# A hybrid decoder step on one core: the down projection's operands split where they are made and brought back by GpSimd's queue

## The chip, the core and the metric

The program runs on one core of a Trainium2 chip. TensorE (PE) multiplies, VectorE (DVE) and ScalarE (ACT) do the elementwise work, GpSimd (POOL) a little of it, and SyncE (SP) issues the transfers between DRAM (HBM) and the core's on-chip memory (SBUF). Products gather in eight banks of PSUM. The metric is the device time of one launch in microseconds (us). The kernel before took 1199.58 us, the median of three runs (1198.73 to 1200.3).

## The reference

One layer of a hybrid decoder, on 1088 tokens (1024 of a prompt and 8 sequences of 8 sampled tokens), 1024 features:

```python
h = rmsnorm(x, norm_mix_pre)
mix = concat([conv(h), pool(h), hgrn2(h), conformer(h)]) @ w_out      # four mixers on the columns of h @ w_in
x = x + rmsnorm(mix, norm_mix_post)
h = rmsnorm(x, norm_ffn_pre)
ff = (silu(h @ w_gate) * (h @ w_up)) @ w_down                         # 1024 -> 2816 -> 1024
x = x + rmsnorm(ff, norm_ffn_post)
```

Everything is float32. The change lies in the last product: its inner dimension of 2816 is 22 tiles of 128 hidden features.

## The kernel before, in words

**Split operands.** A float32 product is made of three faster ones. Each operand is split into a high part (a float32r copy, which ACT makes: CAST) and a low part (the rest, which DVE or POOL makes by a subtraction: TENSOR_TENSOR, line 65 through the helper `TT`), and high by high, high by low and low by high are added in PSUM. Names that end in `h` and `l` (`xh0`, `xl0`) are the two parts of the FFN's input, `wop` holds both parts of a weight tile, `raw` a weight tile as loaded.

**Stages.** Phase 1 (to about 380 us of the trace) is the input projection and the mixers. Phase 2 is the output projection, the norms, and the hidden tiles 16, 17 and 18 for all tokens by plain products (`plain`, line 1288, products on line 1297). A planner writes the order of phase 2 by hand: each step of DVE's work is a generator that tells its cost in us, and `hook` places as much of it under a stretch of products as fits; the steps in `bulk` fill what is left, and `due` holds small steps that have to be done at once.

Phase 3a makes the other hidden tiles, 0 to 15 and 19 to 21, with Strassen's seven products in Winograd's form (`strassen`, products on line 1388), tile after tile, in two streams `pr` = 0 and 1 (each half of the tokens), whose products alternate on PE. One tile is 168 matmuls. Tiles 0 to 15 form eight pairs: after the odd tile of a pair, `pair_sums` (line 1430) makes the seven operands that the down projection's own Strassen products need and stores each to DRAM (`hx`), whole, 128 x 272 per stream. Tiles 16 to 21 go whole to `hd`. In this phase a scheduler orders each engine's instructions.

Phase 3b (`down2`, products on line 1593) is the down projection of the eight pairs in four groups `g` of two pairs, each group in four steps `j` of 84 matmuls, so 16 steps. A group needs 14 operands (`x_item`): the operand is loaded from `hx` by SP's queue into one of three `raw` tiles of 128 x 544, ACT copies the high part into the operand tile, and POOL subtracts the low part (DVE does for half of group 0). In the same stage DVE makes the weights of the next step (`prep_ws`) and adds the products from PSUM to the sums (`acc`, `t`, `x`). Operand tiles lie where the FFN's input lay (`xh0` to `xl7`) and in a pool `px` of 9; `room` lists them, and a tile goes back into `room` when the last product of its group that reads it is issued. Last, the tiles 16 to 21 of `hd` are loaded in chunks and split in the same manner (`h_items`), and are multiplied by plain products (line 1481), with the final norm under them. In phase 3b the order of PE, DVE, ACT and POOL is the order in which the code is written: each `next` is a product, and the `xs.step()` or `hs.step()` behind it is one operand.

## Time and profile before

| what | value |
|---|---|
| time, median of 3 runs | 1199.58 us |
| span of the profiled execution | 1193.7 us |
| what lies around the span (the difference) | 5.9 us |
| busy: PE / DVE / ACT / POOL | 1153.1 / 885.4 / 451.0 / 139.9 us |
| phase 2, about | 380 to 538 us of the span |
| phase 3a, about | 538 to 927 us |
| phase 3b, pairs, about | 927 to 1100 us |
| plain tiles and final norm, about | 1100 to 1194 us |

The span runs from the first to the last instruction of the profiled execution; the page gives no other time of it. A matmul record lasts longer (288 ns) than the distance to the next one, since matmuls are pipelined: the pace is read from the number of matmuls in a stretch, not from their busy time. DVE's records overlap a little too: a 128 x 272 TENSOR_TENSOR shows 0.43 us.

### The profile page before, as it was taken

How to read it: one execution, taken by the hardware profiler on the slowest of the kernel's cores; microseconds unless marked ns; L12 is line 12 of the kernel's file. 1: busy time of each engine (PE TensorE's matmuls, PEld its weight loads, DVE VectorE, ACT ScalarE, POOL GpSimd, SP SyncE). 2: the span in 40 equal slices, each digit the busy share in tenths (PEclk: the TensorE clock that was granted, in tenths of full speed). 3: DMA queues.
4: the chain of work that ended last, by engine and by line, in shares of the span. 5: the costliest groups of instructions: out<-in, count | busy, mean ns of one | idle time of the engine just before them, and what ended most of it. 6: DMA issues, size and time to landing. Idle time of an engine off the chain costs nothing.

```text
span 1193.7 us, 21654 instructions
## 1 busy us (share of the span) xinstructions
PE 1153.1 (97%) x8476; PEld 1116.1 (94%) x8476; DVE 885.4 (74%) x1770; ACT 451.0 (38%) x964; POOL 139.9 (12%) x130
## 2 busy tenths in 40 slices
PE   5999999999999999999999999999999999999995
PEld 4899899998999999999999999999999989999994
DVE  6468979997674678786677576666675679998687
ACT  7534322243264453443333233233334653333321
POOL 1000000000000000000000000000002363447234
PEclk9999999999899999999999999999999999999998
DMA  7011112211135123021323233133234453434732
GB/s 261 34 38 24 36 37 68 41 36 40 30 130 199 39 74 127 24 95 67 115 101 105 70 111 118 60 114 110 91 122 135 141 178 121 137 109 125 259 108 88
DMA packets 93333, 116.89 MB, mean 98 GB/s; under 512 B 23664, under 2 KB 62192, under 8 KB 93232
## 3 DMA queue, kind: packets, MB, share of 16 engines
q1 hardware_dynamic: 93232, 115.52, 30.1%
q8 instruction: 66, 1.08, 0.4%
q14 instruction: 35, 0.29, 0.1%
HBM read 86.61 MB, written 28.88 MB: 97 GB/s over the span
## 4 chain that ended last, share of the span: by engine, by line
PE 81%; DVE 10%; issue 3%; DMA 2%; ACT 2%; POOL 1%; SPq 0%; DVEq 0%; ACTq 0%; POOLq 0%
PE p L1388 30%; PE mm L984 18%; PE p L1116 8%; PE p L1593 7%; PE p L1297 5%; PE p L1481 4%; DVE wop L65 3%; DVE raw L65 2%; PE mm L137 2%; PE sm L798 2%; DVE t L65 1%; DMA raw<-wgu 1%; ACT wop L1007 1%; DVE xl L65 1%; DMA raw<-hx 1%
## 5 line engine op out<-in xcount | busy, mean ns | idle before, releaser
L65 DVE TENSOR_TENSOR wop<-raw,wop 128x512 fp32r<-128x512 f32 (+2 forms) x296 | 210.2, 722 | 137.9 <-ACT wop L1007 127.5
L1007 ACT CAST wop<-raw 128x512 fp32r<-128x512 f32 (+1 forms) x240 | 143.4, 604 | 267.0 <-PE p L1388 151.7
L1388 PE MATMUL p<-xh,wop 128*128 128x272 f32 x1216 | 235.1, 288 | 0.0
L1388 PEld LDWEIGHTS p<-xh,wop 128*128 128x128 f32 x1216 | 193.5, 188 | 0.0
L1388 PE MATMUL p<-t,wop 128*128 128x272 f32 x912 | 179.6, 290 | 1.7 <-DVE u L65 1.6
L984 PE MATMUL mm<-xh,wop 128*128 128x256 f32 (+2 forms) x864 | 178.5, 335 | 0.0
L1388 PE MATMUL p<-xl,wop 128*128 128x272 f32 x608 | 175.6, 289 | 0.0
L1388 PEld LDWEIGHTS p<-t,wop 128*128 128x128 f32 x912 | 145.6, 188 | 2.4 <-DVE u L65 2.4
L984 PEld LDWEIGHTS mm<-xh,wop 128*128 128x128 f32 x864 | 139.5, 190 | 6.6 <-issue 1.1
L1388 PE MATMUL p<-x,wop 128*128 128x272 f32 x456 | 131.4, 288 | 0.0
L1388 PEld LDWEIGHTS p<-xl,wop 128*128 128x128 f32 x608 | 114.4, 188 | 0.0
L1116 PE MATMUL p<-xh,wop 128*128 128x272 f32 x512 | 99.2, 290 | 2.0 <-DVE wop L65 2.0
L984 PE MATMUL mm<-xl,wop 128*128 128x256 f32 (+2 forms) x432 | 99.0, 338 | 0.0
L65 POOL TENSOR_TENSOR x<-raw,x 128x544 fp32r<-128x544 f32 (+3 forms) x18 | 24.9, 1389 | 626.4 <-ACT x L1521 613.1
L65 DVE TENSOR_TENSOR raw<-raw,raw 128x512 f32<-128x512 f32 (+1 forms) x123 | 83.7, 690 | 4.5 <-DMA raw<-wgu 3.3
L1388 PEld LDWEIGHTS p<-x,wop 128*128 128x128 f32 x456 | 85.9, 188 | 0.0
L1593 PE MATMUL p<-xh,wop 128*128 128x272 f32 x456 | 82.1, 288 | 2.3 <-DVE acc L65 1.2
L71 DVE SCALAR_TENSOR_TENSOR y<-u,prm,y 128x1024 f32<-128x1024 f32 (+1 forms) x68 | 82.6, 1224 | 2.2 <-ACT y L570 0.7
L1116 PEld LDWEIGHTS p<-xh,wop 128*128 128x128 f32 x512 | 81.0, 188 | 2.2 <-DVE wop L65 2.2
L1593 PE MATMUL p<-xl,wop 128*128 128x272 f32 x456 | 81.5, 288 | 1.2 <-DVE x L65 0.9
L1297 PE MATMUL p<-xh,wop 128*128 128x272 f32 x384 | 74.1, 289 | 0.0
L1116 PE MATMUL p<-xl,wop 128*128 128x272 f32 x256 | 73.9, 289 | 0.0
(322 smaller groups left out, 2021.0 us busy)
## 6 DMA issues: line engine op xcount, KB each, us to landing
raw<-wgu SPq DMA_DIRECT2D x88, 256.0 KB, 2.7
raw<-hx SPq DMA_DIRECT2D x56, 272.0 KB, 2.7
raw<-win SPq DMA_DIRECT2D x40, 256.0 KB, 3.0
hx<-x SPq DMA_DIRECT2D x64, 136.0 KB, 1.8
raw<-wdn SPq DMA_DIRECT2D x32, 256.0 KB, 2.9
raw<-wdn SPq DMA_DIRECT2D x32, 192.0 KB, 2.9
x<-xT SPq DMA_DIRECT2D x8, 544.0 KB, 6.2
x<-x SPq DMA_DIRECT2D x8, 544.0 KB, 3.0
```

What stands on the lines that cost most here:

```text
L65: (eng or V).tensor_tensor(out, a, b, op)
L71: (eng or V).scalar_tensor_tensor(out=out, in0=a, scalar=s, in1=b, op0=op0, op1=op1)
L137: PE.matmul(ps[c][:, :n], hl[:, wi, kk], X[k][:, o:o + n], start=k == 0 and wi == 0 and X is XH, stop=k == KT - 1 and wi == 1)
L798: PE.matmul(ps[:rows, g * P:(g + 1) * P], kk[:, o:o + rows], qz[hf][:, :, g * 64:(g + 1) * 64], start=True, stop=True, skip_group_check=True)
L984: PE.matmul(ps[c][:, :w], hl[:, wi, kk], X[k][:, o:o + w], start=k == order[0] and wi == 0 and X is XH, stop=k == order[-1] and wi == 1)
L1007: S.copy(hl[:, 0], raw)
L1116: PE.matmul(ps[nt][:, :PW], WO[nt][k // 4][:, wi, kk:kk + P], X[k][:, o:o + PW], start=k == korder[0] and wi == 0 and X is XH, stop=k == k ...
L1297: PE.matmul(ps[r][:, :PW], w[:, wi, (k % 4) * P:(k % 4 + 1) * P], X[k][:, o:o + PW], start=k == 0 and wi == 0 and X is XH, stop=k == KT - ...
L1388: PE.matmul(ps[:, :PW], wop[:, wi, kk * P:(kk + 1) * P], x(kk, xi), start=first and kk == 0 and wi == 0 and xi == 0, stop=kk == 3 and wi == 1,
L1481: PE.matmul(ps[:, :n], wd[:, wi, kk * P:(kk + 1) * P], hops[k][xi][:, o:o + n], start=first and kk == 0 and wi == 0 and xi == 0, stop=not ...
L1593: PE.matmul(ps[:, :PW], ws[name][wi][q], x[:, xi, pr], start=first and q == 0 and wi == 0 and xi == 0, stop=q == 1 and wi == 1, skip_group ...
```

## The change

The program that stores a part now splits it first. `pair_sums` stores the operands of pairs 0 and 1 whole as before, and those of pairs 2 to 7 as two parts: `put_split` has ACT copy the high part into one of three tiles `hi`, has DVE subtract it in place, and SP store both. `hx` and `hd` become twice as wide. `plain` and `strassen` do the same for tiles 16 to 21. In phase 3b an operand of groups 1 to 3 is one transfer of 128 x 1088 (544 KB) from `hx` straight into its operand tile, and each tile of `hd` two such transfers; all of them are issued by POOL's queue. Their `raw` loads by SP, copies on ACT and subtractions on POOL go. `px` has 8 buffers in place of 9, and one operand of group 0 lies in a tile `hx` of another pool. The weights' raw tiles in phase 3b come from `w4` instead of a pool of their own. In phase 2 `put_t1(0)` stands ahead of `split_t(0)`.

```diff
-    px = ctx.enter_context(tc.tile_pool(name="px", bufs=9, side="right", reuse_waits="tile"))
+    px = ctx.enter_context(tc.tile_pool(name="px", bufs=8, side="right", reuse_waits="tile"))
...
                     def post(ps=ps[1], g0=g0, o=o):
-                        hst = T(pm, [P, PW], "sqa", bufs=2)
+                        hst, hi = T(pm, [P, PW], "sqa", bufs=2), T(pm, [P, PW], "hhi", F32R, bufs=2)
                         TT(hst, ps[:, :PW], g0)
-                        SY.dma_start(hd[i][:, o:o + PW], hst)
-                    due.append((0.36, post))
+                        S.copy(hi, hst)
+                        TT(hst.bitcast(F32R), hst, f32(hi), ALU.subtract)
+                        for w, t in enumerate((f32(hi), hst)):
+                            SY.dma_start(hd[i][w][:, o:o + PW], t)
+                    due.append((0.72, post))
...
-    bulk += [split_t(0), put_t1(0), split_t(1)]
+    bulk += [put_t1(0), split_t(0), split_t(1)]
...
+    def put_split(t, to):
+        hi = T(w3, [P, PW], "hi", F32R, bufs=3)
+        S.copy(hi, t)
+        TT(t.bitcast(F32R), t, f32(hi), ALU.subtract)
+        for dst, src in zip(to, (f32(hi), t)):
+            SY.dma_start(dst, src)
...
-            SY.dma_start(hx[p][OPS.index(name)][:, pr * PW:(pr + 1) * PW], t)
+            dst = hx[p][OPS.index(name)].rearrange("p (q c) -> p q c", c=PW)
+            if p < 2:
+                SY.dma_start(dst[:, pr], t)
+            else:
+                put_split(t, [dst[:, 2 * w + pr] for w in range(2)])
...
-    room = [None] * 4 + list(range(8)) + [None] * 3 + list(range(8, 16))
+    room = [None] * 3 + list(range(8)) + ["hx"] + [None] * 3 + list(range(8, 16))
...
         def work(raw):
             i, t = take()
+            if g:
+                GP.dma_start(t, src.bitcast(F32R))
             t = t.rearrange("p (w q c) -> p w q c", w=2, q=2)
-            S.copy(t[:, 0], raw)
-            TT(t[:, 1], raw, f32(t[:, 0]), ALU.subtract, eng=V if g == 0 and e % 2 else GP)
+            if not g:
+                S.copy(t[:, 0], raw)
+                TT(t[:, 1], raw, f32(t[:, 0]), ALU.subtract, eng=V if e % 2 else GP)
             xop2[p, name] = t, i
...
-    def h_items(k):
...
+    def load_h(k):
+        hops[k] = []
+        for w in range(2):
+            hops[k].append(take()[1])
+            GP.dma_start(hops[k][w], hd[k][w].bitcast(F32R))
...
-    rawp.append((hq.enter_context(tc.tile_pool(name="hq", bufs=1, reuse_waits="tile")), 3))
+    rawp.append((w4, 3))
...
-                    if e % 2 and (room[1:] or len(hs.items) % 3 != 1):
-                        hs.step()
+                    if hs and room[1:]:
+                        load_h(hs.pop(0))
```

Over the whole program the instructions change so: DVE 1772 to 1880 (96 subtractions behind `hi`, 12 behind `hhi`), ACT 957 to 1005 (108 casts more, 60 fewer), POOL loses 60 subtractions and has 54 transfers, SP 513 to 561 (108 stores more, 60 loads fewer). PE has the same 8200 matmuls; in phases 3a and 3b they stand in the same order and only read tiles of other names.

Three places in the order. First POOL, where group 1's operands are made, before (an operand tile from a raw tile) and now (an operand tile from DRAM):

```order
L65 TENSOR_TENSOR x_10432<-raw_10250,x_10432 128x544
L65 TENSOR_TENSOR xh_1343_10470<-raw_10300,xh_1343_10470 128x544
L65 TENSOR_TENSOR xl_1346_10508<-raw_10321,xl_1346_10508 128x544
L65 TENSOR_TENSOR xh_1349_10544<-raw_10435,xh_1349_10544 128x544
L65 TENSOR_TENSOR xl_1361_10577<-raw_10473,xl_1361_10577 128x544
```

```order
L1542 DMA x_10855<-hx 128x1088
L1542 DMA xh_1447_10890<-hx 128x1088
L1542 DMA xl_1449_10925<-hx 128x1088
L1542 DMA xh_1451_10958<-hx 128x1088
L1542 DMA xl_1462_10988<-hx 128x1088
```

Between group 0 and the last group POOL now has nothing but such transfers, so each waits for its own tile to be free and for the one ahead of it, and for no other engine's work.

Second DVE in phase 3a, from the second stream's pair sums of a pair to the first sum `u` that the next hidden tile's fifth product releases. Before:

```order
L65 TENSOR_TENSOR x_6460<-x_6460 128x272
L65 TENSOR_TENSOR hst_6896<-x_6460 128x272
L65 TENSOR_TENSOR wop_7170<-raw_7150,wop_7170 128x512
L65 TENSOR_TENSOR t_866_6897<-x_6460,hst_6896 128x272
L65 TENSOR_TENSOR u_889_6991<-p_6944,p_883_6959 128x272
L65 TENSOR_TENSOR raw_7150<-raw_7150,raw_7149 128x512
L65 TENSOR_TENSOR u_890_7005<-p_6962,p_888_6977 128x272
L65 TENSOR_TENSOR wop_7174<-raw_7160,wop_7174 128x512
L65 TENSOR_TENSOR wop_7177<-raw_7152,wop_7177 128x512
L65 TENSOR_TENSOR wop_7180<-raw_7150,wop_7180 128x512
L65 TENSOR_TENSOR u_893_7071<-p_6944,p_883_6959 128x272
```

And now, the end of the same stretch, of another pair:

```order
L65 TENSOR_TENSOR t_961_7533<-x_7068,hst_7532 128x272
L65 TENSOR_TENSOR x_7068<-x_7068,hi_7538 128x272
L65 TENSOR_TENSOR x_7068<-x_7068,hi_7543 128x272
L65 TENSOR_TENSOR wop_7838<-raw_7824,wop_7838 128x512
L65 TENSOR_TENSOR wop_7841<-raw_7816,wop_7841 128x512
L65 TENSOR_TENSOR x_7068<-x_7068,hi_7548 128x272
L65 TENSOR_TENSOR x_7068<-x_7068,hi_7553 128x272
L65 TENSOR_TENSOR hst_7532<-hst_7532,hi_7558 128x272
L65 TENSOR_TENSOR wop_7844<-raw_7814,wop_7844 128x512
L65 TENSOR_TENSOR hst_7532<-hst_7532,hi_7563 128x272
L65 TENSOR_TENSOR u_995_7735<-p_7608,p_985_7623 128x272
L65 TENSOR_TENSOR t_961_7533<-t_961_7533,hi_7568 128x272
```

The rows with `hi` are the new subtractions: 13 of a pair's 14 stand ahead of that `u`, seven of the first stream (above these rows) and six of the second.

Third DVE at the end of phase 2, the operands of phase 3a's products (`x<-x,t` the low parts of `split_t`, `xl<-x,xh` those of `put_t1`, `sqa` the hidden tile's post). Before:

```order
L65 TENSOR_TENSOR x_5222<-x_3512,t_0_664_5220 128x1088
L65 TENSOR_TENSOR xl_12_84<-x_3511,xh_4_76 128x272
L65 TENSOR_TENSOR xl_13_85<-x_3511,xh_5_77 128x272
L65 TENSOR_TENSOR sqa_5252<-p_5185,sq_5218 128x272
L65 TENSOR_TENSOR xl_14_86<-x_3511,xh_6_78 128x272
L65 TENSOR_TENSOR xl_15_87<-x_3511,xh_7_79 128x272
```

Now:

```order
L65 TENSOR_TENSOR xl_14_86<-x_3511,xh_6_78 128x272
L65 TENSOR_TENSOR xl_15_87<-x_3511,xh_7_79 128x272
L65 TENSOR_TENSOR x_5258<-x_3817,t_0_669_5256 128x1088
L65 TENSOR_TENSOR x_5274<-x_3816,t_0_671_5272 128x1088
L65 TENSOR_TENSOR x_5278<-x_3512,t_0_673_5276 128x1088
L65 TENSOR_TENSOR sqa_5292<-p_5221,sq_5254 128x272
L65 TENSOR_TENSOR sqa_5292<-sqa_5292,hhi_5293 128x272
```

`put_t1`'s four subtractions stand ahead of `split_t`'s three, and each post has a second instruction.

More of the change, by code (lines that the diff above doesn't have):

```diff
@@ L1424, in strassen @@
         if i >= 2 * NPAIR:
-            SY.dma_start(hd[i][:, oa:oa + PW], hst[:, 0])
-            SY.dma_start(hd[i][:, ob:ob + PW], hst[:, 1])
+            for e, o in enumerate((oa, ob)):
+                put_split(hst[:, e], [hd[i][w][:, o:o + PW] for w in range(2)])
         elif i % 2:
@@ L1454, in body @@
     XS = [f"x{'hl'[i % 2]}{i // 2}" for i in range(2 * KT)]
[L1455 removed]
+    room = [None] * 3 + list(range(8)) + ["hx"] + [None] * 3 + list(range(8, 16))
     def take():
         i = room.pop(0)
[L1460 removed]
+        if i is None:
+            t = T(px, [P, 4, PW], "x", F32R).rearrange("p a b -> p (a b)")
+        else:
+            t = T(hp, [P, NT], i, F32R) if i == "hx" else T(xp, [P, NT], XS[i], F32R)
         return i, t
@@ L1511, in x_item @@
         p, name = 2 * g + e % 2, OPS[e // 2]
+        src = hx[p][OPS.index(name)]
         def begin():
+            if g:
+                return None
             raw = T(w4, [P, 2 * PW], "raw", bufs=3).rearrange("p (q c) -> p q c", c=PW)
-            SY.dma_start(raw, hx[p][OPS.index(name)].rearrange("p (q c) -> p q c", c=PW))
+            SY.dma_start(raw, src[:, :2 * PW].rearrange("p (q c) -> p q c", c=PW))
             return raw
@@ L1519, in work @@
             i, t = take()
+            if g:
+                GP.dma_start(t, src.bitcast(F32R))
             t = t.rearrange("p (w q c) -> p w q c", w=2, q=2)
-            S.copy(t[:, 0], raw)
-            TT(t[:, 1], raw, f32(t[:, 0]), ALU.subtract, eng=V if g == 0 and e % 2 else GP)
+            if not g:
+                S.copy(t[:, 0], raw)
+                TT(t[:, 1], raw, f32(t[:, 0]), ALU.subtract, eng=V if e % 2 else GP)
             xop2[p, name] = t, i
         return begin, work
-    def h_items(k):
-        def item(c):
-            o, n = DC[c]
-            def begin():
-                raw = T(w4, [P, 2 * PW], "raw", bufs=3)[:, :n]
-                SY.dma_start(raw, hd[k][:, o:o + n])
-                return raw
-            def work(raw):
-                if c == 0:
-                    hops[k] = [take()[1] for _ in range(2)]
-                hi, lo = (h[:, o:o + n] for h in hops[k])
-                S.copy(hi, raw)
-                TT(lo, raw, f32(hi), ALU.subtract, eng=GP)
-            return begin, work
-        return [item(c) for c in range(len(DC))]
+    def load_h(k):
[3 more added lines that the diff above has]
+            GP.dma_start(hops[k][w], hd[k][w].bitcast(F32R))
     def load_ws(g, j):
@@ L1624, in body @@
     xs = Stream([x_item(g, e) for g in range(NGP) for e in range(14)], 3)
-    hs = Stream([i for k in range(16, NF) for i in h_items(k)], 3)
+    hs = list(range(16, NF))
     wsp = [{} for _ in order]
@@ L1635, in body @@
         if i == rest[-3]:
-            for _ in range(3):
+            for _ in range(2):
                 begin, work = xs.items.pop(0)
@@ L1650, in body @@
     hp = ctx.enter_context(tc.tile_pool(name="hp", bufs=1, reuse_waits="tile"))
+    xs.step(1)
     acc = [T(tpp, [P, 4, PW], f"t{j % 3 + 2}_{j // 3}").rearrange("p a b -> p (a b)") for j in range(6)]
@@ L1683, in body @@
             del prep[:]
-        while hs.items or hs.raws:
-            hs.step()
-    hq.close()
-    rawp[-1] = w4, 3
-    hq.close()
-    rawp[-1] = w4, 3
+        while hs:
+            load_h(hs.pop(0))
     hf = ctx.enter_context(tc.tile_pool(name="hf", bufs=1, reuse_waits="tile"))
```

4 lines of the change are left out of this document (1 added, 3 removed).

## The prediction

> **What bounds the kernel now.** I read the busy shares of the page first, then busy time by stage, then PE's waits in the stage that falls short, then the groups by shape in two stages beside each other.
>
> ```profile
> PE 1153.1 (97%) x8476; PEld 1116.1 (94%) x8476; DVE 885.4 (74%) x1770; ACT 451.0 (38%) x964; POOL 139.9 (12%) x130
> ```
>
> PE is the bound nearly everywhere; a change to other engines can only give back what PE loses. The table by stage (length, then PE, PEld, DVE, ACT, POOL with instructions in brackets, clock, transfer share, GB/s) shows where it loses:
>
> ```profile
> 440.00:480.00 40.00, 40.00 (x323) 40.00 (x323) 33.59 (x85) 15.22 (x35) 0.00 (x0) 1.00 0.40 134
> 480.00:540.00 60.00, 58.19 (x455) 56.87 (x453) 47.03 (x88) 26.13 (x54) 0.00 (x0) 1.00 0.18 61
> 540.00:900.00 360.00, 359.88 (x2861) 359.66 (x2862) 242.01 (x495) 112.43 (x224) 2.71 (x2) 1.00 0.29 98
> 640.00:680.00 40.00, 40.00 (x320) 40.00 (x320) 27.09 (x57) 12.24 (x25) 0.00 (x0) 1.00 0.28 96
> 920.00:960.00 40.00, 39.66 (x317) 39.44 (x316) 27.76 (x52) 25.18 (x60) 16.10 (x11) 1.00 0.53 160
> 960.00:1000.00 40.00, 37.25 (x292) 36.45 (x292) 35.09 (x70) 17.35 (x37) 20.37 (x15) 1.00 0.46 144
> 1000.00:1040.00 40.00, 37.83 (x299) 37.17 (x298) 38.06 (x78) 15.38 (x28) 20.60 (x14) 1.00 0.50 151
> 1040.00:1080.00 40.00, 38.81 (x311) 38.59 (x310) 38.21 (x80) 13.67 (x28) 16.98 (x15) 1.00 0.31 96
> 945.00:1085.00 140.00, 133.89 (x1056) 132.20 (x1056) 126.15 (x252) 57.91 (x118) 71.70 (x55) 1.00 0.44 135
> ```
>
> In phase 3a PE has no gap: 320 matmuls in 40 us, 0.125 us each. In phase 3b, from 960 to 1080, it has 292, 299 and 311, 58 fewer than 960: 7.3 us, and 0.4 us more from 920 to 960. There DVE is at 35 to 38 of 40. What PE waited for from 945 to 1085 (total, times, longest):
>
> ```profile
> PE p L1593 <- DVE t L65: 2.7, 3, 1.5
> PE p L1593 <- DVE acc L65: 2.4, 2, 1.2
> PE p L1593 <- DVE x L65: 0.9, 1, 0.9
> ```
>
> All is DVE, 6.0 us as gaps. Why DVE is full there is in its groups by shape, first in 540:900, where POOL is idle, then in 945:1085 (count, busy, mean ns of one, idle before):
>
> ```profile
> L65 DVE TENSOR_TENSOR wop<-raw,wop 128x512 fp32r<-128x512 f32 x120 | 83.2, 695 | 95.0 <-ACT wop L1007 94.8
> L65 DVE TENSOR_TENSOR raw<-raw,raw 128x256 f32<-128x256 f32 x2 | 0.8, 421 | 0.0
> ```
>
> ```profile
> L65 DVE TENSOR_TENSOR wop<-raw,wop 128x512 fp32r<-128x512 f32 x38 | 33.5, 881 | 9.3 <-ACT wop L1007 8.8
> L65 DVE TENSOR_TENSOR raw<-raw,raw 128x256 f32<-128x256 f32 x37 | 25.9, 725 | 0.4
> L65 DVE TENSOR_TENSOR wop<-raw,wop 128x256 fp32r<-128x256 f32 x12 | 9.2, 765 | 1.5 <-ACT wop L1572 1.5
> L65 DVE TENSOR_TENSOR raw<-raw 128x256 f32<-128x256 f32 x13 | 7.6, 583 | 0.0
> L65 POOL TENSOR_TENSOR xl<-raw,xl 128x544 fp32r<-128x544 f32 x14 | 21.1, 1509 | 30.3 <-ACT xl L1521 28.4 <-PE p L1593 1.9
> L65 DVE TENSOR_TENSOR t<-p,t 128x272 f32<-128x272 f32 x102 | 39.8, 430 | 1.1 <-PE p L1593 0.9
> ```
>
> Subtractions with two inputs in SBUF are longer beside POOL's: 881 against 695 ns, 725 against 421. Those that read PSUM (`t<-p,t`) keep their 430. So POOL's splits hold DVE up, and DVE holds PE.
>
> **The change, part by part.** *Phase 3b, taken away:* POOL's splits. At the undisturbed length DVE saves 38 x 0.186 = 7.1 us, 37 x 0.304 = 11.2, 12 x 0.34 = 4.1 and 13 x 0.16 = 2.1 (the last two against 421): 24.5 us. DVE falls from 126.2 to 101.7 of 140 us, 73%, near the 67% (242 of 360) at which phase 3a lost nothing. Of PE's 7.7 us I take nine tenths, 6.9; bounds: half, 3.8, if POOL's issuing still disturbs DVE, and all 7.7. ACT loses 60 copies where it had time: nothing.
>
> Whether POOL's issuing disturbs DVE no row shows. By the Trainium skill, page "SBUF — State Buffer", section "Who interferes with whom", a DVE instruction with two SBUF inputs contends with a GpSimd instruction that reads SBUF and not with one that only writes it; the trace agrees on the first half (881 against 695 ns, and `t<-p,t` unharmed). By that rule, descriptors that are only written leave DVE alone and the sum would hold all 24.5 us. Against the change, the section "SBUF: two separate sides" warns that DVE in a two-port mode keeps GpSimd from writing descriptors, so such transfers stand still.
>
> *Phase 3b, added:* 42 transfers of 544 KB and 12 of `hd`, on POOL's queue. The trace has no transfer issued there; the nearest rows (size, median us to landing) are
>
> ```profile
> x<-xT SPq DMA_DIRECT2D x8, 544.0 KB, 6.2
> x<-x SPq DMA_DIRECT2D x8, 544.0 KB, 3.0
> raw<-hx SPq DMA_DIRECT2D x56, 272.0 KB, 2.7
> hx<-x SPq DMA_DIRECT2D x64, 136.0 KB, 1.8
> hx<-t SPq DMA_DIRECT2D x16, 136.0 KB, 2.7
> ```
>
> so 3.0 to 6.2 us; I take 5, nearer to the load. Nine of a group's 14 operands find room a group ahead. The other five need tiles that the last step's first three products free, and are read by the next step's fifth to seventh: ten products of six matmuls in two streams lie between, 10 x 12 x 0.125 = 15 us. In the window 1000:1040, 151 GB/s took a share of 0.50: 300 GB/s at most. Five transfers are 2.8 MB, 9 us, plus some 3 us to land: 12 of 15. On average a group's 42 us carry 7.8 MB of operands and 2.1 MB of weights, 236 GB/s or a share of 0.8. It fits, with little to spare: 0. POOL's later additions (`add_p1`) stand behind `hd` transfers whose tiles were freed a group ago: 0.
>
> *Phase 3a, added:* 84 splits in pairs and 12 more, each a copy on ACT, a subtraction on DVE and one store more on SP. Their place is the end of a pair. DVE there now:
>
> ```profile
> 650.33 0.44 DVE L65 TENSOR_TENSOR hst<-x 128x272 f32<-128x272 f32 x1
> ...
> 652.34 0.43 DVE L65 TENSOR_TENSOR x<-u,c 128x272 f32<-128x272 f32 x1
> 652.69 0.43 DVE L65 TENSOR_TENSOR t<-x,hst 128x272 f32<-128x272 f32 x1
> 653.04 0.43 DVE L65 TENSOR_TENSOR hst<-x 128x272 f32<-128x272 f32 x1
> ...
> 657.04 0.69 DVE L65 TENSOR_TENSOR wop<-raw,wop 128x512 fp32r<-128x512 f32 x1 [0.21 <-ACT wop L1007]
> 660.03 0.69 DVE L65 TENSOR_TENSOR wop<-raw,wop 128x512 fp32r<-128x512 f32 x1 [2.30 <-ACT wop L1007]
> 663.40 0.69 DVE L65 TENSOR_TENSOR wop<-raw,wop 128x512 fp32r<-128x512 f32 x1 [2.67 <-ACT wop L1007]
> 664.01 0.43 DVE L65 TENSOR_TENSOR u<-p,p 128x272 f32<-128x272 f32 x1
> ```
>
> One subtraction costs 0.35 us from start to start. The 13 that stand ahead of the next tile's `u` at 664.01 cost 4.6 us; DVE's idle time before it is 0.2 + 2.3 + 2.7 = 5.2 us. So they fit by 0.6 us, if each finds its copy done. Those come from ACT through three `hi` tiles, each busy until its store has landed: a copy (0.4 us), the subtraction and 1.8 to 2.7 us, 2.6 to 3.5 us a round, and the last 11 of 14 need 3.7 rounds, 9.5 to 13 us of the 13.7 us from 650.33, where the first pair sum starts, to `u`. A late copy holds DVE, behind it `u`, and `u` holds the bank that PE's next product of that stream adds to, due one product of the other stream (1.5 us) after `u` is called for. Per pair I take 0.25 us, six pairs 1.5; bounds 0 and 1.5 us a pair, 9. The 12 extra splits of tiles 19 to 21 spread over three tiles: 0.
>
> SP has 28 stores a pair for 14, and weight loads stand behind stores that wait for a subtraction. What covers them is that weights are early:
>
> ```profile
> L1007 ACT CAST wop<-raw 128x512 fp32r<-128x512 f32 x119 | 73.7, 620 | 157.8 <-PE p L1388 146.5 <-DVE raw L65 8.9 <-DMA raw<-wgu 2.4
> ```
>
> ACT's copies of weights wait 146.5 us for PE to free a tile and 2.4 for a load: 0. One `px` buffer less means that a pair's sums have only the two that the pair before used; they are written 168 x 0.125 = 21 us after that pair's burst begins, and its stores are out by then: 0.
>
> *Phase 2, added:* 12 copies and subtractions, 12 x 0.35 = 4.2 us of DVE, which idles 6.4 us in 440:480 and 13 in 480:540 while PE works. The planner counts 0.36 us more for each, so other steps move back. PE lost 1.8 us in 480:540; the new order may keep, lose or add to it: -1.2 to +2.5, taken as 0.5.
>
> Sum: -6.9 + 1.5 + 0.5 = -4.9 us on the profiled span of 1193.7, so 1188.8. The span lies 5.9 us below the median of the runs, and what is around it stays: 1194.7.
>
> **The rivals.** *A, half the gain:* POOL's writing of descriptors takes DVE's port as its subtractions did, some 1 us in place of 1.5 each, and the transfers number 54 for 60. Gain 3.8, costs 2: 1197.8, no measurable change. For it: that DVE and POOL do share something is plain; against: POOL would read nothing.
>
> *B, slower, the end of a pair:* if stores land in 2.7 us and ACT's silu copies (which wait for PE) stand between the `hi` copies, the burst runs past `u` by 1.5 us in each of six pairs: +9 - 6.9 + 0.5, 1202.2. It decides from 0.8 us a pair on (6 x 0.8 + 0.5 = 5.3 leaves 1.6). For it: 13.0 of 13.7 us at the slow store; against: DVE is idle 33% there, and ACT 69%.
>
> *C, slower, late operands:* POOL's queue moves less than SP's. From 2.8 MB in 12 us, 230 GB/s, downwards the five operands miss their 15 us; at 200 GB/s each of three group changes waits 2 us, 1200.7; at 150 GB/s 7.8 MB take 52 us of a group's 42, three groups 30 us, 1224.7. For it: no row has this queue; against: a whole tile moves in rows of 4 KB, the same bytes by the same engines. The Trainium skill's warning above ("SBUF — State Buffer", "SBUF: two separate sides") would give the same by another way, transfers that stand still; its "Who interferes with whom" names no two-port mode for TENSOR_TENSOR, the only DVE instruction of phase 3b.
>
> **How the numbers follow.** The forecast gets 0.63, A 0.14, B 0.12, C 0.11. Its own range is 1190.7 (all 7.7 us, phase 2 at its best) to 1198. The whole range, 1190.5 to 1203, takes in A and B and leaves out most of C and the far ends, about 0.16. A measurement here tells 0.2%, 2.4 us, from no change: faster 0.63, same 0.15 (A and a little of B), slower 0.22.
>
> **What would show it.** Right: in phase 3b PE at 315 or more matmuls in each 40 us, `raw<-raw,raw` 128x256 back near 421 ns, DVE below 33 of 40; in 3a PE still near 320 with DVE near 31. Wrong: PE waiting for DVE `u` at every second tile of 3a (B); PE waiting for `x`, `xh` or `xl` from DRAM at the first step of a group (C); `raw<-raw,raw` still above 600 ns with POOL's queue busy (A); a gap of more than 2 us at the end of phase 2.

## The result, and the profile after

The changed kernel took 1205.57 us (median, 1201.92 to 1206.36) where the kernel before took 1199.57 (1198.73 to 1200.3): a ratio of 1.0056, 95% interval 1.0037 to 1.0076. Beside other kernels on another occasion it took 1206.41 us against 1197.07, 1.008 (1.006 to 1.010). The change makes the kernel slower by 0.6 to 0.8%; the prediction said 1194.7 and gave 1190.5 to 1203.

Where it went, by the first and last matmul of each stage in the profiled executions (us; the last column is the corrected version, to which the experiments led):

| stage | before | after | difference | corrected |
|---|---|---|---|---|
| plain products of phase 2 | 77.3 | 82.1 | +4.8 | 77.1 |
| phase 3a | 403.9 | 414.0 | +10.1 | 405.4 |
| phase 3b, pairs | 176.8 | 170.3 | -6.5 | 170.0 |
| from there to the end | 91.2 | 93.0 | +1.8 | 93.0 |
| span | 1193.7 | 1204.6 | +10.9 | 1187.1 |

(Ahead of the plain products lie 441 to 446 us that the change does not touch; they differ that much between executions. The stage figures come from one profiled execution of each kernel; of the changed kernel there are two, and their stages differ by at most 0.7 us.) By these matmuls phase 3a of the kernel before starts at 522 us, and not at about 538 as the table ahead of the prediction has it, so the window 480:540 takes in its first 18 us. The span of the profiled execution of before was a low one: where both are known, the run is 2.0 us longer than its span before the change and 1.8 after, so 1193.7 belongs to a run of about 1195.7. The medians are 6 to 9 us apart, the two spans 10.9.

Busy time by stage, after (the stretches that the prediction showed of before):

```profile
480.00:540.00 60.00, 56.45 (x430) 55.01 (x429) 47.56 (x96) 27.25 (x57) 0.00 (x0) 0.97 0.19 64
540.00:900.00 360.00, 353.73 (x2789) 351.98 (x2788) 262.73 (x566) 138.15 (x305) 1.39 (x1) 1.00 0.38 127
640.00:680.00 40.00, 38.69 (x308) 38.48 (x308) 30.07 (x67) 15.88 (x37) 0.00 (x0) 1.00 0.43 144
960.00:1000.00 40.00, 40.00 (x322) 40.00 (x322) 26.12 (x61) 16.48 (x39) 7.39 (x14) 1.00 0.77 272
1000.00:1040.00 40.00, 40.00 (x322) 40.00 (x322) 35.03 (x85) 7.36 (x14) 7.38 (x14) 1.00 0.67 229
1040.00:1080.00 40.00, 40.00 (x322) 40.00 (x321) 35.15 (x84) 8.28 (x16) 7.00 (x14) 1.00 0.67 230
```

Phase 3b runs at the full pace, 322 matmuls in 40 us for 292 to 311. Phase 3a, which had no gap, has lost 72 of 2861 matmuls between 540 and 900. The groups of DVE in 945:1085 show the relief:

```profile
L65 DVE TENSOR_TENSOR t<-p,t 128x272 f32<-128x272 f32 x98 | 41.8, 438 | 8.0 <-PE p L1603 6.3
L65 DVE TENSOR_TENSOR wop<-raw,wop 128x512 fp32r<-128x512 f32 x40 | 27.6, 689 | 12.0 <-ACT wop L1007 11.6
L65 DVE TENSOR_TENSOR raw<-raw,raw 128x256 f32<-128x256 f32 x40 | 16.2, 431 | 0.5
```

689 ns for 881, 431 for 725, and 438 for 430 where one input is in PSUM: without POOL's subtractions, DVE's are as short as in phase 3a before (695 and 421). The price is in the waits of 530:930, phase 3a (total, times, longest), first two lines of before, then the changed kernel:

```profile
DVE raw L65 <- DMA raw<-wgu: 3.3, 3, 1.8
PE p L1388 <- DVE u L65: 1.6, 2, 1.2
```

```profile
ACT hi L1437 <- DMA hx<-hi: 23.8, 24, 3.6
ACT hi L1437 <- DVE x L65: 16.9, 12, 4.3
DVE hst L65 <- ACT hi L1437: 13.8, 8, 3.9
DVE raw L65 <- DMA raw<-wgu: 9.1, 7, 2.2
PE p L1391 <- DVE u L65: 7.9, 8, 2.2
```

The first, third and fifth of these lines are a chain: the copy into `hi` waits until the store of a `hi` tile has landed in DRAM, DVE's subtraction waits for the copy, and PE waits for the `u` that stands behind the subtraction on DVE. The end of one pair shows it in order of time (the first `hst<-x`, the first pair sum, is at 654.34):

```profile
655.56 0.73 ACT L1437 CAST hi<-x 128x272 fp32r<-128x272 f32 x2
...
659.30 0.42 ACT L1437 CAST hi<-t 128x272 fp32r<-128x272 f32 x1 [0.38 <-DMA hx<-hi]
...
662.54 0.40 SPq L1440 DMA_DIRECT2D hx<-hi  x1
...
663.18 0.42 ACT L1437 CAST hi<-x 128x272 fp32r<-128x272 f32 x1 [2.16 <-DMA hx<-hi]
...
668.01 0.42 ACT L1437 CAST hi<-hst 128x272 fp32r<-128x272 f32 x1 [1.75 <-DMA hx<-hi]
...
668.46 0.44 DVE L65 TENSOR_TENSOR hst<-hst,hi 128x272 fp32r<-128x272 f32 x1 [1.66 <-ACT hi L1437]
...
669.63 0.42 ACT L1437 CAST hi<-t 128x272 fp32r<-128x272 f32 x1
...
670.23 0.43 DVE L65 TENSOR_TENSOR u<-p,p 128x272 f32<-128x272 f32 x1
```

Thirteen copies lie between 655.56 and 670.05. The first three found tiles free; the other ten took 12.8 us, 3.8 us a round of three. The copy of 659.30 is done at 659.72, and its store is issued at 662.54: it stands behind four others on SP, the first of which is in issue for 1.6 us, the rest some 0.5 us apart. So a tile's round is copy, turn on SP's queue and landing. Over all 96 copies, each set beside its store in the trace, the turn took 0.6 us on average (at most 3.3) and the landing 2.5 (median 1.9, one in ten 3.8 or more), so that a tile was held for 3.5 us on average. The `u` of 670.23 (the next tile's `u3`, which PE's product `t4` waits for) came 13.7 us after the first pair sum in the kernel before; here it comes after 15.9.

The longest of PE's gaps costs more than its own length. PE in stretches of 2 us after the end of the next pair:

```profile
712.00:714.00 2.00, 1.22 (x10) 0.99 (x8) 0.46 (x2) 1.27 (x4) 0.00 (x0) 1.00 0.26 88
714.00:716.00 2.00, 0.56 (x2) 0.57 (x3) 2.00 (x6) 1.21 (x3) 0.00 (x0) 0.78 0.64 225
716.00:718.00 2.00, 2.00 (x11) 2.00 (x10) 1.38 (x4) 0.00 (x0) 0.00 (x0) 0.50 0.75 238
718.00:720.00 2.00, 2.00 (x16) 2.00 (x15) 0.88 (x2) 0.42 (x1) 0.00 (x0) 0.87 0.83 263
```

PE stands from 713.2 to 715.4, and then the granted clock is 0.50 for some 3 us: 39 matmuls in 8 us where 64 fit, 3.1 us for a gap of 2.2.

Phase 2 after, in order of time (`rs_b1` is the chain of small steps that makes a norm's factor, `x<-x,prm,p` applies it, `xh` and `xl` are then what PE's next products read):

```profile
483.15 0.16 DVE L65 TENSOR_TENSOR rs_b1a<-rs_b1a,rs_b1h 128x3 f32<-128x3 f32 x1
484.36 0.44 DVE L65 TENSOR_TENSOR sqa<-p,sq 128x272 f32<-128x272 f32 x1 [1.05 <-PE p L1297]
484.83 0.42 ACT L1308 CAST hhi<-sqa 128x272 fp32r<-128x272 f32 x1 [1.63 <-DVE sqa L65]
...
485.28 0.44 DVE L65 TENSOR_TENSOR sqa<-sqa,hhi 128x272 fp32r<-128x272 f32 x1 [0.48 <-ACT hhi L1308]
485.64 0.15 DVE L71 SCALAR_TENSOR_TENSOR rs_b1y<-rs_b1a,rs_b1y 128x3 f32<-128x3 f32 x1
...
486.30 1.31 DVE L71 SCALAR_TENSOR_TENSOR x<-x,prm,p 128x272 f32<-128x272 f32 x3
486.82 1.23 ACT L1182 CAST xh<-x 128x272 fp32r<-128x272 f32 x3 [1.57 <-DVE x L71]
```

The norm's chain stands for 2.3 us while DVE waits for PE's product, multiplies, waits for ACT's copy, and subtracts. PE then waits 2.7 us for `xh`, and the clock drops here too:

```profile
485.00:490.00 5.00, 2.14 (x10) 1.51 (x10) 4.62 (x15) 2.40 (x7) 0.00 (x0) 0.98 0.17 57
490.00:495.00 5.00, 5.00 (x28) 4.66 (x28) 2.46 (x7) 1.57 (x4) 0.00 (x0) 0.68 0.00 0
```

### The profile page after: what moved, and what is told of

It reads as the page before. It is cut to its first block, busy times and chain, and to the rows that moved or that the text cites. A ratio compares the mean times of both kernels' runs of the same rounds, so it can differ in the third digit from the quotient of the medians.

```text
span 1204.6 us, 21947 instructions
## 1 busy us (share of the span) xinstructions
PE 1156.3 (96%) x8476; PEld 1118.7 (93%) x8476; DVE 898.9 (75%) x1878; ACT 458.3 (38%) x1012; POOL 88.3 (7%) x124
## 4 chain that ended last, share of the span: by engine, by line
PE 82%; DVE 7%; DMA 6%; ACT 3%; issue 1%; POOL 0%; SPq 0%; ACTq 0%; DVEq 0%; POOLq 0%
PE p L1391 26%; PE mm L984 16%; PE p L1603 13%; PE p L1116 8%; PE p L1297 6%; PE p L1499 4%; DMA hx<-hi 2%; PE mm L137 2%; PE sm L798 1%; DMA raw<-win 1%; DVE wop L65 1%; DVE hst L65 1%; DMA conv_s<-u 1%; ACT wop L1007 1%; DVE xl L65 1%
## 5 line engine op out<-in xcount | busy, mean ns | idle before, releaser
L65 DVE TENSOR_TENSOR wop<-raw,wop 128x512 fp32r<-128x512 f32 (+2 forms) x296 | 195.8, 675 | 91.3 <-ACT wop L1007 80.1
L1391 PE MATMUL p<-t,wop 128*128 128x272 f32 x912 | 182.8, 292 | 8.5 <-DVE u L65 8.5
L65 DVE TENSOR_TENSOR raw<-raw,raw 128x512 f32<-128x512 f32 (+1 forms) x123 | 70.7, 585 | 10.3 <-DMA raw<-wgu 9.1
L65 DVE TENSOR_TENSOR t<-p,t 128x272 f32<-128x272 f32 (+3 forms) x138 | 60.3, 449 | 18.8 <-PE p L1499 9.0
## 6 DMA issues: line engine op xcount, KB each, us to landing
xl<-hx POOLq DMA_DIRECT2D x15, 544.0 KB, 10.2
```

Of the source, the lines that this page charges most:

```text
L65: (eng or V).tensor_tensor(out, a, b, op)
L1391: PE.matmul(ps[:, :PW], wop[:, wi, kk * P:(kk + 1) * P], x(kk, xi), start=first and kk == 0 and wi == 0 and xi == 0, stop=kk == 3 and wi == 1,
```

## Experiments on phase 3a

Three theories of its 10.1 us. **R, the ring:** copies wait for one of three `hi` tiles to land, DVE waits in order behind the copies, and `u` behind DVE. **S, SP's queue:** 28 stores a pair for 14 make the weights' loads late. **D, the work:** 14 subtractions more per pair on DVE are too many in any case. All kernels here are the changed kernel with the edit shown; ratios are to the kernel before, run beside them (1195.8 to 1197.1 us).

### One tile more, one tile less

```diff
-        hi = T(w3, [P, PW], "hi", F32R, bufs=3)
+        hi = T(w3, [P, PW], "hi", F32R, bufs=4)      # the other kernel: bufs=2
```

> One more `hi` tile (four for three) in `put_split`; nothing else. Three theories of the 10 us that phase 3a lost (403.9 to 414.0 us). R, the ring: a copy waits until one of three `hi` tiles has landed in DRAM (ACT waited 23.8 us in 24 waits for that), DVE waits in order behind it and holds the next `u`. R expects the waits of `hi` for landings to fall by a third or more and 3a to get back 3 to 6 us: 1200 to 1203 us. S, SP's queue: 28 stores stand in order on it and the loads of weights behind them; S expects no change, within 1.5 us of 1205.6. D, DVE's own work: 14 subtractions more per pair, 4.9 us, are too many in any case; D expects no change.

> One `hi` tile less (two for three); nothing else. R expects 14 copies in seven rounds of 2.6 to 3.5 us for 4.7 rounds, 6 to 8 us later in each of six pairs, of which most is PE's: phase 3a 20 us longer or more, 1225 us or above. S expects within 3 us of 1205.6, since the stores set the pace. D expects within 2 us.

Four tiles: 1196.99 us, 1.0015 (1.0005 to 1.0026), phase 3a 408.8 us. Two tiles: 1208.42 us, 1.010 (1.008 to 1.012), 3a 414.9 (and phase 3b 173.4 for 170.3). The waits in 530:930, with four and with two:

```profile
ACT hi L1437 <- DMA hx<-hi: 16.9, 28, 1.9
PE p L1391 <- DVE u L65: 4.2, 5, 2.1
```

```profile
ACT hi L1437 <- DMA hx<-hi: 54.0, 40, 3.5
PE p L1391 <- DVE u L65: 9.7, 8, 2.1
```

With four, 3a got back 5.2 us, as R said and neither S nor D allow; the waits for landings fell by 29%, a little less than the third that R asked for. Two did not do what R said (20 us longer): ACT waits more than twice as long, but PE hardly more than with three, and S's forecast, within 3 us of 1205.6, held for this run. The order of DVE gives a reason. In phase 3a a scheduler makes it, and it came out differently: with three tiles, 13 of a pair's 14 subtractions stand ahead of the next tile's `u3`, with two tiles 10. With two, fewer stand in its way, and the rest are late behind it. R's forecast for this run left the order as it was. No run keeps the order and takes the tile away, so this reason is read from the order and not shown.

### Stores without the split

```diff
-        hi = T(w3, [P, PW], "hi", F32R, bufs=3)
-        S.copy(hi, t)
-        TT(t.bitcast(F32R), t, f32(hi), ALU.subtract)
-        for dst, src in zip(to, (f32(hi), t)):
+        for dst, src in zip(to, (t, t)):
```

> `put_split` stores the tile twice and leaves out the copy and the subtraction, so the down projection gets wrong low parts; the bytes and the number of stores are the same. R and D expect phase 3a back at about 404 us, so 1195 to 1197 us in all. S expects 3a to keep at least half of its loss, 408 us or more, 1200 us or above. Between R and D this run does not decide.

The kernel leaves out the split and stores each operand whole, twice. 1195.7 us, 0.9999 (0.998 to 1.0015): the total as R and D expected, phase 3a, at 408.0 us, as S did. With no copy and no subtraction, 3a keeps 4.1 us. After the pair that ends at 862 the loads of weights are issued at 875.95, 14 us after the tile's product (`x<-g,p`, 861.90), and in the kernel before 8.3 us after it (867.34 and 859.01). There DVE waits 3.7 us for such a load, and PE's longest gap of this phase (1.94 us) ends with the `u` behind it. So in this kernel S's mechanism costs PE time.

### SP relieved, in three ways

```diff
             # put_split; three kernels, each with one of these
-            SY.dma_start(dst, src)
+            GP.dma_start(dst, src)                              # all stores on POOL's queue
+            (S if src is not t else SY).dma_start(dst, src)     # the high parts' stores on ACT's queue
             # load_hidden
-            SY.dma_start(blk[b], wgu[i][:, b])
+            (GP if 0 < i < 16 or i > 18 else SY).dma_start(blk[b], wgu[i][:, b])   # weights on POOL's queue
```

> The stores of `put_split` are issued by POOL's queue instead of SP's, which is idle in phase 3a; nothing else. S expects the weights' loads to be no later than before the change and 3a to get back 5 to 10 us: 1196 to 1201 us. R expects what the landing gives: the stores no longer stand behind each other's waits, but if a store issued by POOL lands later than 1.9 us, the ring turns slower: 1205 to 1215 us. D expects no change, 1204 to 1207.

> The stores of the high parts in `put_split` are issued by ACT's queue, right behind the copy that makes them; SP keeps the stores of the low parts, 14 a pair as before the change. Three `hi` tiles as in the changed kernel. S, SP's queue (the stores that have no copy and no subtraction behind them kept 4.1 us of the 10 that phase 3a lost, and their 28 issues took 13.5 us on SP before the weights' loads): 3a gets back 4 us or more, 410 us or less. R, the ring: a high part's store no longer stands behind the low part before it, so it lands sooner and 3a gets back 4 to 8 us too. If only the copies and subtractions count, 3a stays at 413 to 415 us. A cost of its own would show as ACT's other copies being late, with PE waiting for them.

> The loads of the gate and up weights of phase 3a are issued by POOL's queue, so they stand behind no store; the 28 stores of a pair stay on SP, with three `hi` tiles. S expects DVE's waits for weight loads (9.1 us) to fall to those of the kernel before (3.3) and 3a to get back 4 us or more: 410 us or less. R expects 3a within 2 us of 414, since the copies wait for landings as before. If loads issued by POOL are late by themselves (those of 544 KB took 9.5 to 10.2 us to land, against 3.1 for 256 KB on SP), 3a gets longer than 416 us and DVE's waits for loads grow.

None of the three took phase 3a to 410 us or less: 430.1, 418.2 and 433.4 us; 1224.11, 1203.84 and 1221.86 us in all, 1.024, 1.008 (1.005 to 1.010) and 1.022. (The profiled execution with the stores on ACT's queue was the longest of its kernel, 1210.3 us; its median is 2.6 us below that of the changed kernel beside it, so that its 3a is longer as a rule is not shown.) DVE's waits for weights did fall, from 9.1 us to 2.1, 2.1 and 2.2, so S's mechanism is there, but behind the pairs it is not what PE waits for. What grew is the landing. The DMA issues in 530:930, of the stores on POOL's queue, on ACT's queue, and on SP's beside weights on POOL's:

```profile
hx<-hi POOLq DMA_DIRECT2D x84, 136.0 KB, 2.6
```

```profile
hx<-hi ACTq DMA_DIRECT2D x84, 136.0 KB, 3.0
```

```profile
hx<-hi SPq DMA_DIRECT2D x84, 136.0 KB, 2.8
```

The stores land in 2.6 to 3.0 us for 1.9, and on POOL each issue also takes 0.54 us of POOL itself, 15 us for the 28 of a pair that has 13.7. With POOL's queue, ACT waited 41.2 and 40.5 us for landings, and R's "slower if stores land later" held, with a size (16 and 19 us) that none had given. With ACT's own queue it waited 19.0 us, less than the changed kernel's 23.8, and what the 4 us in the 3a of that execution are is not shown; nor was it pursued why stores of two queues land later. S's forecast failed with POOL's queue, twice, by 20 us and more.

### The ring without landings

```diff
-        for dst, src in zip(to, (f32(hi), t)):
+        for dst, src in zip(to, (t, t)):
```

> Copies, subtractions and the number and bytes of the stores are those of the changed kernel, but both stores of an operand bring its low part: the high parts of the operands made in phase 3a never reach DRAM, so the down projection gets wrong values, and a `hi` tile is free as soon as the subtraction has read it. R, the ring (a copy waits until a `hi` tile has landed): phase 3a falls from 414 to 406 to 409 us, near the 408.0 of the kernel that stores without splitting. D, DVE's and ACT's added work: 3a stays at 412 us or more. That SP's queue matters was not borne out (two ways of taking issues off it left 3a at 418 and 433).

1194.13 us, 0.9983 (0.997 to 0.9997), phase 3a 405.2 us. PE's waits for `u`:

```profile
PE p L1391 <- DVE u L65: 1.7, 3, 0.8
```

This kernel stores the low part twice and never the high part; all copies and subtractions and all 28 stores are there, and 8.8 of the 10.1 us are gone, a little more than R asked for. So D is at most 1.3 us, and the 4.1 us of the stores alone were no fixed price of 28 stores. Here all 14 subtractions of a pair stand ahead of the next tile's `u3`, and it comes 13.6 us after the first pair sum, as in the kernel before (13.7), where the changed kernel has 14.7 to 16.8.

### One store for both parts

```diff
             # put_split; its two callers (left out here) name one place for both parts
-        hi = T(w3, [P, PW], "hi", F32R, bufs=3)
-        S.copy(hi, t)
-        TT(t.bitcast(F32R), t, f32(hi), ALU.subtract)
-        for dst, src in zip(to, (f32(hi), t)):
-            SY.dma_start(dst, src)
+        hl = T(w3, [P, 2, PW], "hi", F32R, bufs=2)
+        S.copy(hl[:, 0], t)
+        TT(hl[:, 1], t, f32(hl[:, 0]), ALU.subtract)
+        SY.dma_start(to, f32(hl))
```

> Both parts of an operand are made in one tile of 2 x 272 (two such tiles, the room of four single ones) and leave by one store of 272 KB: 14 stores a pair on SP, as before the change, and one wait for a landing per operand. R with the landing as its price: two tiles, each busy for copy, subtraction and landing (2.6 to 3.5 us), make 14 operands in 18 to 24 us, slower than three single tiles: 3a at 416 us or more. If instead it is the number of stores and what they hold up, 3a falls to 410 or less.

Phase 3a took 410.1 us, near the lower of the two forecasts (410 or less) and not R's 416 or more: half the stores, no turn behind a low part, but ACT waited 51.5 us for landings that now took 2.7 us. So the landing alone is not the ring's price. The whole took 1208.39 us, 1.009 (1.007 to 1.012), since phase 3b rose to 178.8, where PE has a wait of 8.2 us for an ACT copy; that was not pursued.

### The subtraction on POOL

```diff
-        TT(t.bitcast(F32R), t, f32(hi), ALU.subtract)
+        TT(t.bitcast(F32R), t, f32(hi), ALU.subtract, eng=GP)
```

> The subtractions of `put_split` go to POOL, which is idle in phase 3a; three `hi` tiles. D, and R in so far as DVE waits in order behind a late copy, expect DVE free for `u`: waits of PE for `u` below 3 us (8.5 to 8.9 in the changed kernel), 3a at 404 to 408 us. Against it: POOL took 1.5 us for twice the size, so a ring tile is held 0.4 us longer, and DVE's subtractions with two SBUF inputs get longer beside POOL's (881 for 695 ns in phase 3b of the kernel before). If that decides, 3a stays at 412 us or more and `wop<-raw,wop` 128x512 in 3a shows 730 ns or more for 695.

1215.79 us, 1.015 (1.010 to 1.019), phase 3a 428.3. DVE and POOL in 530:930:

```profile
L65 DVE TENSOR_TENSOR wop<-raw,wop 128x512 fp32r<-128x512 f32 x130 | 94.2, 732 | 75.8 <-ACT wop L1007 75.3
L65 POOL TENSOR_TENSOR x<-x,hi 128x272 fp32r<-128x272 f32 x48 | 42.6, 905 | 531.6 <-ACT u L1423 377.7 <-DVE x L65 112.2 <-issue 29.3
```

0.9 us on POOL for 0.43 on DVE, so a tile is held longer and ACT waited 39.9 us for landings; and DVE's subtractions with two inputs in SBUF rise from 695 to 732 ns. Although POOL had been idle in this phase and DVE is rid of the work, 3a is 14 us longer in this execution (1220.3 us; the median is 9 to 10 us above the changed kernel's): relieving DVE gains nothing here. How much of this is the ring and how much DVE's longer subtractions was not separated.

### A ring of ten places

Three of a stream's seven operands take tiles that the finished hidden tile no longer needs, so the ring grows without room:

```diff
-    def put_split(t, to):
-        hi = T(w3, [P, PW], "hi", F32R, bufs=3)
+    def put_split(t, to, tag=None):
+        hi = T(w3, [P, PW], tag, bufs=2).bitcast(F32R) if tag else T(w3, [P, PW], "hi", F32R, bufs=4)
...
-                put_split(t, [dst[:, 2 * w + pr] for w in range(2)])
+                put_split(t, [dst[:, 2 * w + pr] for w in range(2)], {"b21": "u3", "t2": "g0", "t4": "c22"}.get(name))
```

> Ten places for the ring: four `hi` tiles, and for three of a stream's seven operands (`b21`, `t2`, `t4`) the tiles `u3`, `g0` and `c22`, which the odd tile of the pair has done with and the next tile needs 10 to 15 us later. Everything else, the high parts' stores too, as in the changed kernel; phase 2 untouched. R expects nearly all that the ring without landings got back (405.2 us): 3a at 405 to 408, ACT's waits for landings below 8 us (23.8 with three, 16.9 with four), 0.999 to 1.002 of the kernel before. If four tiles had got what a ring can get back (408.0 and 408.8), 3a stays at 408 to 410.

1194.43 us, 0.998 (0.9968 to 0.9992), phase 3a 404.9 us, with all parts stored. Waits in 530:930:

```profile
DVE raw L65 <- DMA raw<-wgu: 10.0, 7, 3.0
ACT hi L1437 <- DMA hx<-hi: 2.6, 3, 1.3
PE p L1391 <- DVE u L65: 2.4, 3, 1.6
```

Landings are down from 23.8 us to 2.6 and PE's waits for `u` from 7.9 to 2.4, while DVE's waits for weights are as in the changed kernel. R is shown both ways: by leaving out the landing, and by making the ring large enough.

The matmuls of phase 3a stand in the same order in all these kernels, so their start times can be set beside those of the kernel before, tile by tile. What each stretch takes longer, in us (the second column holds the tile that follows each of the six split pairs):

| kernel | first tile | six tiles behind a pair | hidden tile 20 | last tile | phase 3a |
|---|---|---|---|---|---|
| changed | -1.5 | 9.3 (0.4 to 3.8 each) | 2.0 | 0.3 | 10.1 |
| changed, second execution | -1.5 | 8.0 | 3.9 | 0.4 | 10.8 |
| four `hi` tiles | -1.5 | 2.2 | 3.9 | 0.3 | 4.9 |
| ring without landings | -1.0 | -0.4 | 2.3 | 0.3 | 1.2 |
| ring of ten | -1.2 | 0.1 | 1.9 | 0.3 | 1.0 |

All other tiles take the same time to 0.01 us. So the loss behind the pairs is the ring's altogether, D is nothing there, and two things remain outside the pairs. The first tile gains since the kernel before has a gap of 1.2 us there, behind a late load of weights. Tile 20 loses in the changed kernel like this:

```profile
902.21 0.40 SPq L1440 DMA_DIRECT2D hd<-hst  x1
902.66 0.44 SPq L1235 DMA_DIRECT2D raw<-wgu  x1
905.99 2.20 DVE L65 TENSOR_TENSOR raw<-raw,raw 128x512 f32<-128x512 f32 x3 [2.17 <-DMA raw<-wgu]
913.03 0.39 PE L1391 MATMUL p<-t,wop 128*128 128x272 f32 x1 [1.60 <-DVE u L65]
```

The load of weights stands behind six stores of tile 19's split parts, DVE waits for it, and PE for a `u` behind that: S's mechanism. Tile 20 loses nothing where the stores do not wait for a split, where one store carries both parts, where ACT's queue has half of them, and where POOL's queue has the loads; where POOL's queue has all the stores it still loses 1.9 us, so the cause is likely and not shown. The ring of ten does not cure it.

## Experiments on phase 2

```diff
     # hook: what is due is taken once, and may leave a step for the next place
-        for cost, fn in due:
+        now = due[:]
+        due.clear()
+        for cost, fn in now:
             fn()
             state["budget"] -= cost
-        due.clear()
...
                         S.copy(hi, hst)
-                        TT(hst.bitcast(F32R), hst, f32(hi), ALU.subtract)
-                        for w, t in enumerate((f32(hi), hst)):
-                            SY.dma_start(hd[i][w][:, o:o + PW], t)
-                    due.append((0.72, post))
+                        SY.dma_start(hd[i][0][:, o:o + PW], f32(hi))
+
+                        def low():
+                            TT(hst.bitcast(F32R), hst, f32(hi), ALU.subtract)
+                            SY.dma_start(hd[i][1][:, o:o + PW], hst)
+                        due.append((0.36, low))
+                    due.append((0.36, post))
...
-    for cost, fn in due:
-        fn()
-    due.clear()
+    while due:
+        due.pop(0)[1]()
```

> The changed kernel once more, beside the others of this set, so that they have one to stand against. In the first set the kernel before had a median of 1195.8 us and executions from 1194 to 1202. Expected from the first comparison (1.0056): 1202.5 us, between 1200 and 1206.

> Phase 2 only: the split of a plain tile is two steps, the product with the high part's copy and store at once, the subtraction and the low part's store at the next place that takes such steps, so that DVE no longer waits for ACT's copy between the two. If the 4.8 us of phase 2 come from these waits (0.5 us each, ahead of the chain of small steps that makes the norm's factor), the plain products take 78 to 80 us for 82, 2 to 4 us less in all. If it is the added 4.2 us of DVE's work in a stretch that is full, they stay at 81 to 83. Phase 3a stays at 414.

The changed kernel beside it took 1206.41 us (1.008), just above what was expected, with stages as in the first execution (82.0, 414.7, 170.1). Two steps: 1201.26 us, 1.003 (1.0014 to 1.0046). The plain products took 80.9 us, 1.1 less: below what the theory of waits asked for, and not nothing. Phase 3a came out at 411.1 for 414.7, which the edit does not touch. Of this, 2.5 us lie in tile 20, where PE's gap is 2.1 us in the one, with a slow clock behind it, and 1.0 us in the other; why is not known.

> The two edits that helped, together: four `hi` tiles, and the plain tiles' split in two steps. Against the kernel before, the one measured 1.0015 and the other 1.003, the changed kernel 1.0056 and 1.008. If they act in different stages the gains add: 1.0068 less 0.0053 less 0.0038, 0.998 (0.995 to 1.001), with the plain products at about 81 us, 3a at 406 to 409 and 3b at 170. If they meet in 3a, 1.001 to 1.003.

1195.2 us, 0.9993 (0.998 to 1.001); plain products 80.5, phase 3a 408.0: the gains add.

> The changed kernel without the split of the plain tiles in phase 2: their products are stored whole, twice, at the planner's old cost, so the down projection gets wrong low parts of tiles 16 to 18; the order of `put_t1(0)` and `split_t(0)` and the smaller `px` stay. If phase 2's 4.8 us come from the split, the plain products are back at 77 to 78 us and the whole is 4 to 6 us below the changed kernel (1.001 to 1.004 of the one before). If they come from the order, they stay at 80 or more.

```diff
-                        S.copy(hi, hst)
-                        TT(hst.bitcast(F32R), hst, f32(hi), ALU.subtract)
-                        for w, t in enumerate((f32(hi), hst)):
-                            SY.dma_start(hd[i][w][:, o:o + PW], t)
-                    due.append((0.72, post))
+                        for w in range(2):
+                            SY.dma_start(hd[i][w][:, o:o + PW], hst)
+                    due.append((0.36, post))
```

The kernel leaves out the split of these tiles: plain products 77.3 us, 1201.79 us, 1.0038 (1.0026 to 1.005). So the split makes phase 2's loss, and neither the changed order nor the smaller `px` does.

> The same ring, and the plain tiles' split in two steps. Four tiles with two steps measured 0.9993 (0.9979 to 1.0008); 1 to 3 us less in 3a gives 0.997 to 0.9985, 1192.5 to 1194.5 where the kernel before has 1196.

> The same, and the plain tile's product step one place later, when its products are finished. In the two-step kernel DVE still waited 5.9 us in three waits for PE at this step, ahead of the norm's chain of small steps, and PE lost its pace at 480 to 490. If this wait is what is left of phase 2's loss, the plain products take 78 to 79 us for 80.5 to 80.9: 1.5 to 2.5 us less than the kernel beside it. If DVE's added work is, no change between the two.

The edit of the second, on top of the two steps and the ring of ten:

```diff
-                    due.append((0.36, post))
+                    due.append((0.0, lambda post=post: due.append((0.36, post))))
```

Two steps with the ring of ten: 1191.73 us, a little below the forecast, 0.996 (0.9946 to 0.9974), plain products 80.6, phase 3a 403.8. With the product step one place later: **1188.87 us, 0.9932 (0.9919 to 0.9944)**, plain products 77.1, more than the 1.5 to 2.5 us expected. All added work is still there. DVE's waits for ACT's copy in 440:528, with the change and in this kernel:

```profile
DVE sqa L65 <- ACT hhi L1308: 6.6, 11, 1.2
DVE sqa L65 <- ACT hhi L1309: 0.8, 2, 0.5
```

The same window of time in this kernel:

```profile
480.00:540.00 60.00, 59.53 (x469) 58.56 (x468) 50.23 (x103) 27.40 (x56) 0.00 (x0) 1.00 0.23 76
```

469 matmuls for 430 with the change and 455 before it, with DVE busier (50.2 us) than in either. (The window holds 3 to 9 us more of phase 3a here; the plain products themselves took 77.1, 82.1 and 77.3 us.) So DVE's added 4.2 us were never too many. What cost 4.8 us was that DVE, in order, waited for PE and ACT at these steps, ahead of a chain that PE waited for. This version beats both kernels.

## Why the prediction was wrong

**Phase 3b, gain -6.9 (3.8 to 7.7): right.** It gained 6.5 us by the reason given; subtractions with two inputs in SBUF went back to 689 and 431 ns (421 expected) and PE to 322 in 40 us. By the Trainium skill, page "SBUF — State Buffer", section "Who interferes with whom", a DVE instruction with two SBUF inputs contends with a GpSimd instruction that reads SBUF and not with one that only writes it; the trace agrees: POOL's queue issued all these transfers and DVE kept its lengths, while POOL's subtractions in phase 3a lengthened them again (732 ns). No run takes POOL's subtractions away and leaves the rest; the lengths and PE's pace are what shows it. One sign failed in part: DVE was at 35 of 40 us in two of the three windows, not below 33, and PE lost nothing with it.

**Transfers of phase 3b, 5 us to land (3.0 to 6.2): wrong and harmless.** They took 9.1 to 10.2:

```profile
xh<-hx POOLq DMA_DIRECT2D x16, 544.0 KB, 9.5
xl<-hx POOLq DMA_DIRECT2D x15, 544.0 KB, 10.2
```

The 5 us taken from the nearest rows, transfers of the same size on SP's queue, were short by half; the trace before also has a row of 512 KB at 7.4 us (`y<-xn`), outside the range. The bytes were no limit: 272 GB/s at a share of 0.77 are 353 GB/s for the whole, where the prediction had 300 at most. PE waited for none of these transfers: nine of 14 operands have a whole group's time, and the other five 15 us for some 10. The sum's 0 for this part held, and rival C fell.

**Phase 3a, +1.5: the step that failed**, with +10.1, past the upper bound of 9. The mechanism was in the prediction; the cost of a pair's end was mis-sized, 0.25 us for a measured 0.4 to 3.8, 9.3 us for the six. Three things made it so. The round of a `hi` tile was taken as 2.6 to 3.5 us from copy, subtraction and landing; the store's turn on SP's queue, 0.6 us on average and up to 3.3, was not counted, and the round came out at 3.5 on average, the slow end, and at 3.8 in the pair shown. The paragraph on SP asked only for the weights behind its stores, and not whether the ring waits there itself. The copies were given the whole 13.7 us from the first pair sum on; in the pair shown the third copy ended 2.9 us after that sum, so ten copies had 10.8 us, and a round above 3.2 us was late already. And with 13 of 13.7 us at the slow end by its own working, a figure near the lower bound was chosen. Of a late `u` PE then lost all but 0.4 to 0.6 us, and behind the longest gap the slow clock made it 1.4 times the gap, which no part of the sum held.

Two smaller terms of 3a failed too. The 12 extra splits of tiles 19 to 21, put at 0, go with 2.2 us in tiles 20 and 21; weights were called early for phase 3a as a whole, and there they were not. And 1.5 us came back in the first tile: PE's gap there is 1.2 of the 1.8 us that the prediction saw lost in 480:540 and counted under phase 2. Rival B, with a chance of 0.12, was this case, and its 1.5 us a pair came out (9.3 in six); its total of 1202.2 did not, since phase 2 and tile 20 came on top.

**Phase 2, +0.5 (-1.2 to +2.5): the second step that failed**, +4.8. It compared 4.2 us of added subtractions with DVE's idle time. The corrected version, which has all of these subtractions, shows that this comparison was right and beside the point: the loss lay in where DVE waits (6.6 us in 11 waits for ACT's copy of `hhi`, by the waits of 440:528) and in what stands behind.

**The tail, nothing: +1.8.** Of this, 1.6 us lie behind the last instruction of an engine, which ends 2.6 us before the end of the span before and 4.2 after. It is 2.7 again where POOL's queue also carried stores or weights in 3a; neither the instructions nor the transfers show what it is. That stays open.

**The base.** The 5.9 us "around the span" set a short execution against the median of others; it is 2.0. With it the same sum would have said 1190.8, further from the result.

With both repaired, the parts come near the forecast's: -6.8 for 3b, +1.5 for 3a and -0.2 for phase 2 by the corrected version's stages, -5.5 for the -4.9 of the sum. (Its median is 7.5 us below the kernel before, its span 6.6; +1.8 of that is the tail, and -2.9 lies ahead of the plain products.) That 3a comes out at the forecast's +1.5 is luck: it is -1.5 in the first tile, 0.8 behind the pairs, 1.9 in tile 20 and 0.3 in the last. The direction was right for the idea, and wrong for the change as it was written.

## What to carry to other kernels

A ring of tiles that are stored from is held for the copy, the turn on the issuing queue and the landing; count rounds with all three, and where they nearly fill the time, look for tiles that are already dead rather than for a faster queue. Work that fits into an engine's idle time by its length can still stop it: on an in-order engine ask what each added step waits for and what stands behind it, and place it where its inputs are ready. A gain won in one stage by moving work to another is paid there, at the first wait that the moved work brings along.
